# GpSimd's low-part subtractions in pieces of 512 columns

## The chip, the core and the metric

The kernel runs on one core of one Trainium2 chip. The metric is the device time of one execution in microseconds (us); the number to predict is the median over several runs. The engines are called as in the profile: PE is TensorE's matmul, PEld its weight load, DVE is VectorE, ACT is ScalarE, POOL is GpSimd, and SP issues the DMAs.

## What is computed

Two decoder layers over 1024 tokens of 1024 features, in float32. The first layer's mixer selects 256 keys for each token with an indexer (top-k) and attends to them through a latent; the second is a sliding-window attention with grouped keys. Each layer also reads a memory of 256 tokens through a cross-attention, and is followed by a gated MLP with a short causal convolution.

```python
for i in range(DEPTH):                                   # 2 layers: mixer A, then mixer B
    h = rmsnorm(x, g_mix[i])
    mix, q_mem = mixer_a(h, ...) if kind == 0 else mixer_b(h, ...)
    mem_o = memory_cross_attention(q_mem, mem_n, w_mem_kv[i])
    x = x + jnp.concatenate([mix, mem_o], axis=-1) @ w_out
    x = x + conv_glu_ffn(rmsnorm(x, g_ffn[i]), f_w_up[i], f_conv_w[i], f_conv_b[i], f_w_down[i])
return rmsnorm(x, g_final)
```

## The kernel before

Everything lies with features on the 128 partitions and tokens along the columns, in two halves of 512 tokens (`HT`). Float32 accuracy comes from splitting: a value is rounded to `float32r` by ACT (the high part, a copy), and the low part is value minus high part. A product is then three matmuls (`mm3`, lines 256 to 258): high by high, high by low, low by high. The third, L258, reads the low part of the weights as the stationary operand, 128 columns at a time.

The weights come as units of 128 x 1024 (`ukv`: 896). `Weights._split` (lines 92 to 108) takes a loaded unit, has ACT copy the high part (L99) and POOL subtract (L100), some units ahead of their use (`SPLIT`). For the second layer's up projection the units are factors of 128 x 512 that DVE forms first; their copy is L105, their subtraction L106. A projection (`proj`) reads a unit in eight blocks of 128 columns, three matmuls for each; the down products read two units together, four pairs of blocks one after the other into PSUM tiles of 128 x 1024, and each is added to the residual by DVE (L852 in the first layer, L1040 in the second), which frees the PSUM tile.

Other subtractions on POOL: `norm_apply`'s inner `lower` (L447), where every second block of the normalized activations goes to POOL and the others to DVE; `store_hl` (L555) for the rotated queries; `gate` (L806) and `keep` (L941) in the MLPs, each of 512 columns; and `split` (L273).

DVE has the rest: the sums of squares of a norm (`fold_in`, L393 and L401: folds of 1024 columns into 512, and additions of blocks), whose result PE multiplies with ones (L413); Newton's steps for the reciprocal root (L416 to L428, on 128 x 4); the normalization (L455); and the top-k search of the first layer, a bisection over bits with very small operations (L1229 to L1272, on 128 x 4 or smaller) between counts over the scores (L1224).

The program is issued by hand in one order (`manual_schedule`): each engine runs its instructions in the order in which Python issued them. Work in the background is interleaved by estimated times (`tick`, `add_bg`); those estimates don't depend on how many instructions a subtraction is made of. All DMAs are issued on SP's queue. All 128 x 4 KB tiles (`t4`) come from one pool of 51 buffers.

Of the kernel before, what the change touches and what calls it, by code (L numbers as in the profile page):

```python
# [59 lines left out]
class Weights:  # L60
# [30 lines left out]
    def _split(self):  # L91
        i = self.ready
        while self.loaded < self.need[i]:
            self._load()
        nc, t = self.t.nc, self.t
        if len(self.order[i]) == 2:
            raw, w = self.raw.pop(self.need[i] - 1)
            hi, lo = t.t4(1024, dt=R32), t.t4(1024, dt=R32)
            nc.scalar.copy(hi[:, :w], raw[:, :w])  # L99
            nc.gpsimd.tensor_tensor(lo[:, :w], raw[:, :w], hi[:, :w].bitcast(F32), op=OP.subtract)  # L100
            self.hl[i] = (hi, lo)
        else:
            src = self._factor(i)
            hl = t.t4(2, HT, dt=R32)
            nc.scalar.copy(hl[:, 0], src)  # L105
            nc.gpsimd.tensor_tensor(hl[:, 1], src, hl[:, 0].bitcast(F32), op=OP.subtract)  # L106
            self.hl[i] = (hl[:, 0], hl[:, 1])
        self.ready += 1

# [64 lines left out]
class Trunk:  # L174
# [85 lines left out]
    def evac_hl(self, hi, lo, src, scale=1.0):  # L260

        nc = self.nc
        if scale == 1.0:
            nc.scalar.copy(hi, src)  # L264
            nc.vector.tensor_tensor(lo, src, hi.bitcast(F32), op=OP.subtract)  # L265
        else:
            nc.scalar.mul(hi, src, scale)
            nc.vector.scalar_tensor_tensor(lo, src, scale, hi.bitcast(F32), op0=OP.mult, op1=OP.subtract)

    def split(self, hi, lo, src):  # L270

# [167 lines left out]
    def norm_apply(self, rb, x, gain, per, out, pace=2500, ease=False, keep=None, engs=None):  # L439


        nc, hs = self.nc, []

        def lower(i, h, hi):
            lo = self.t4(1024, dt=R32).rearrange("p (k n) -> p k n", k=per)
            eng = engs or (nc.gpsimd if i % 2 else nc.vector)
            eng.tensor_tensor(lo, h, hi.bitcast(F32), op=OP.subtract)  # L447
            out.append((hi, lo))

        late = []  # L450
        for i in range(len(x) + 1):
            if i < len(x):
                h = self.t4(1024).rearrange("p (k n) -> p k n", k=per)
                for k in range(per):
                    nc.vector.scalar_tensor_tensor(h[:, k], x[i][:, k], gain[:, i * per + k:i * per + k + 1], rb,  # L455
                                                   op0=OP.mult, op1=OP.mult)
                hs.append(h)
                if keep:
                    keep(i, h)
                yield pace  # L460
            if late:
                lower(*late.pop())
            if i:
                h = hs.pop(0)
                hi = self.t4(1024, dt=R32).rearrange("p (k n) -> p k n", k=per)
                nc.scalar.copy(hi, h)
                late.append((i - 1, h, hi))
                if not ease:
                    lower(*late.pop())
        if late:  # L470
            yield 1200
            lower(*late.pop())
# [77 lines left out]
    def store_hl(self, key, src, dst, scale=1.0, in_sbuf=False):  # L550

        hi, lo = self.t4(2, HT, dt=R32)[:, :, :src.shape[-1]], self.t4(2, HT, dt=R32)[:, :, :src.shape[-1]]
        if in_sbuf:
            self.nc.scalar.copy(hi, src)
            self.nc.gpsimd.tensor_tensor(lo, src, hi.bitcast(F32), op=OP.subtract)  # L555
        else:
            self.evac_hl(hi, lo, src, scale)
        for e in range(2):
            self.store(key, dst(0, e), hi[:, e].bitcast(F32))
            self.store(key, dst(1, e), lo[:, e].bitcast(F32))  # L560
# [213 lines left out]
    def ffn(self, l, halves, fold=1, last=None, then=None):  # L774
# [24 lines left out]
        def gate(f, hf, uv, b):  # L799
            u, v = uv  # L800
            nc.vector.tensor_tensor(u, v, b, op=OP.mult)
            if f % 2 == 0:
                G[hf, f // 2] = (self.t4(2, HT, dt=R32), self.t4(2, HT, dt=R32))
            gh, gl = G[hf, f // 2]
            nc.scalar.copy(gh[:, f % 2], u)
            nc.gpsimd.tensor_tensor(gl[:, f % 2], u, gh[:, f % 2].bitcast(F32), op=OP.subtract)  # L806

        def up(f):
            wa = self.w.get(f"up{l}", f)
# [109 lines left out]
    def ffn_up(self, l, h, ready, B, n_std, near_end):  # L919

        nc, name = self.nc, f"up{l}"

        def conv(f, hf, a):
            cw, prev = self.conv[:, l, f], self.prev_a[:, l, f]
            u = self.t4(HT)
            nc.scalar.activation(u, a, AF.Identity, bias=cw[:, 3:4], scale=cw[:, 2:3])
            nc.vector.scalar_tensor_tensor(u[:, 1:], a[:, :HT - 1], cw[:, 1:2], u[:, 1:], op0=OP.mult, op1=OP.add)
            nc.vector.scalar_tensor_tensor(u[:, 2:], a[:, :HT - 2], cw[:, 0:1], u[:, 2:], op0=OP.mult, op1=OP.add)  # L930
            if hf == 0:
                nc.scalar.copy(prev, a[:, HT - 2:])
            else:
                nc.vector.scalar_tensor_tensor(u[:, 0:1], prev[:, 1:2], cw[:, 1:2], u[:, 0:1], op0=OP.mult, op1=OP.add)
                nc.vector.scalar_tensor_tensor(u[:, 0:2], prev, cw[:, 0:1], u[:, 0:2], op0=OP.mult, op1=OP.add)
            return u

        def keep(f, hf, u):
            t = self.t4(2, HT, dt=R32)
            nc.scalar.copy(t[:, 0], u)  # L940
            nc.gpsimd.tensor_tensor(t[:, 1], u, t[:, 0].bitcast(F32), op=OP.subtract)  # L941
            self.store("G", self.G_d[f][hf], t.bitcast(F32))

        for hf in range(2):
            while not ready(hf):
                self.tick(100)
            for f in range(n_std):
                a, b = self.psB(), self.psB()
                self.proj(a, self.w.get(name, f), h[hf])
                u = conv(f, hf, a)  # L950
                wb = self.w.get(name, NF + f)
                if hf and f == n_std - 1:
                    self.w.SPLIT = self.AHEAD
                self.proj(b, wb, h[hf])
                nc.scalar.activation(u, u, AF.Silu)
                nc.vector.tensor_tensor(u, u, b, op=OP.mult)
                keep(f, hf, u)
                del a, b, u, wb
        b11, b21, b22 = h[0][:2], h[0][2:], h[1][2:]
        del h[:]  # L960
        while len(B[3]) < 2:
            self.tick(100)

        def group(f):
            A, Bk, C = self.psB(), self.psS()[:, :HT], self.psB()
            k = [0]

            def mul(out, b, start):
                w = self.w.get(name, (f, NF + f), k[0])
                k[0] += 1  # L970
                self.product(out, w, b, start)

            tt = nc.vector.tensor_tensor
            cu, vc, ab = self.t4(2, HT), self.t4(2, HT), self.t4(2, HT)
            c1, u2, v, c22, c12, c21 = cu[:, 0], cu[:, 1], vc[:, 0], vc[:, 1], ab[:, 0], ab[:, 1]
            mul(A, b11, True)
            nc.scalar.copy(c1, A)
            yield
            mul(Bk, B[1], True)
            tt(u2, c1, Bk, op=OP.add)  # L980
            yield
            mul(C, B[0], True)
            tt(v, c1, C, op=OP.add)
            yield
            mul(A, b21, False)
            ua = conv(f, 0, A)
            yield
            mul(Bk, B[2], False)
            tt(c22, v, Bk, op=OP.add)
            nc.scalar.activation(ua, ua, AF.Silu)  # L990
            yield
            mul(C, b22, False)
            tt(c12, u2, C, op=OP.add)
            ub = conv(f, 1, c12)
            yield
            mul(Bk, B[3], False)
            tt(c21, c1, Bk, op=OP.add)
            tt(ua, ua, c21, op=OP.mult)
            nc.scalar.activation(ub, ub, AF.Silu)
            yield  # L1000
            keep(f, 0, ua)
            tt(ub, ub, c22, op=OP.mult)
            yield
            keep(f, 1, ub)

        before = iter(())
        for f in range(n_std, NF):
            g = group(f)
            for _ in range(7):
                next(g)  # L1010
                next(before, None)
            for _ in before:
                pass
            before = g
            near_end(f)
        for _ in before:
            pass
        self.w.SPLIT = Weights.SPLIT
# [1108 lines left out]
```

## Time and profile before

| | |
|---|---|
| median of 3 runs | 2682.89 us (2682.31 to 2684.56) |
| profiled execution, its own time | 2683.7 us |
| its span, first to last instruction | 2681.9 us |
| mean granted TensorE clock | 0.965 |
| DVE busy | 1775.3 us (66%) |
| ACT busy | 1190.1 us (44%) |

The profile is of one execution. Busy times are unions of an engine's instructions. A timeline merges instructions that follow each other with the same line and shape (x2, x3) and gives the time from the first one's start to the last one's end; "[4.11 <-DVE t L852]" means that the engine had been idle for 4.11 us before it, and that the wait was ended by the instruction of line 852 on DVE that writes a tile t. pS and pB are PSUM tiles, t is any of the SBUF tiles.

### The profile page before, as it was taken

To read this page: it belongs to the slowest core of one execution; us is meant where nothing else is said; L and a number is where in the kernel's file an instruction comes from. 1 tells how busy PE (TensorE), PEld (TensorE's weight loads), DVE (VectorE), ACT (ScalarE), POOL (GpSimd) and SP (SyncE) were. 2 spreads that over 40 slices of the span, in tenths; PEclk is the share of its full clock that TensorE was granted. 3 is DMA by queue.
4 is the path that set the end of the run, shared out by engine and by line. 5 is a ranking of instruction groups with operands and counts; after the bars stand their busy time and mean duration, and the time that the engine had idled before them with its cause. 6 is when DMAs were issued, how large, how long until landed. Compare 5 with 4: busy or idle time off the path is not lost. (4 is left out here: it accounts for less than half of the span.)

```text
span 2681.9 us, 33704 instructions
## 1 busy us (share of the span) xinstructions
PE 2480.3 (92%) x11912; PEld 2066.6 (77%) x11912; DVE 1775.3 (66%) x3016; ACT 1190.1 (44%) x2214; POOL 1344.5 (50%) x942
## 2 busy tenths in 40 slices
PE   6789889988998999989999989999989999999997
PEld 5667667867776789877778878878867888887886
DVE  7899997876679556664663361588786565655446
ACT  4444456644442555433333333678744444442103
POOL 4544343444554643336756555656645666664203
PEclk8899999998998999999999999999999999999998
DMA  5444345422222254232323327453144323249301
GB/s 198 145 150 133 127 135 209 148 72 88 84 85 74 77 201 126 87 118 79 104 84 110 102 75 235 136 187 115 67 157 157 120 101 124 97 145 365 134 24 63
DMA packets 122233, 338.00 MB, mean 126 GB/s; under 512 B 13136, under 2 KB 30032, under 8 KB 122064
## 3 DMA queue, kind: packets, MB, share of 16 engines
q1 hardware_dynamic: 122064, 335.85, 37.4%
q8 instruction: 94, 1.54, 0.2%
q14 instruction: 75, 0.61, 0.1%
HBM read 262.40 MB, written 73.40 MB: 125 GB/s over the span
## 5 line engine op out<-in xcount | busy, mean ns | idle before, releaser
L100 POOL TENSOR_TENSOR t<-t,t 128x1024 fp32r<-128x1024 f32 (+1 forms) x292 | 720.6, 2483 | 483.1 <-ACT t L99 328.9
L256 PE MATMUL pB<-t,t 128*128 128x512 f32 (+3 forms) x1824 | 683.1, 375 | 12.0 <-DVE t L766 4.7
L257 PE MATMUL pB<-t,t 128*128 128x512 f32 (+3 forms) x1824 | 680.3, 373 | 11.6 <-DVE t L447 9.4
L258 PE MATMUL pB<-t,t 128*128 128x512 f32 (+3 forms) x1824 | 680.1, 373 | 8.9 <-POOL t L100 8.9
L256 PE MATMUL pS<-t,t 128*128 128x512 f32 (+1 forms) x1460 | 578.7, 396 | 59.5 <-DVE t L852 28.0
L258 PE MATMUL pS<-t,t 128*128 128x512 f32 (+1 forms) x1460 | 572.7, 392 | 13.1 <-POOL t L100 13.1
L257 PE MATMUL pS<-t,t 128*128 128x512 f32 (+1 forms) x1460 | 572.6, 392 | 0.8 <-DVE t L498 0.8
L256 PEld LDWEIGHTS pB<-t,t 128*128 128x128 f32 (+1 forms) x1824 | 347.0, 190 | 73.3 <-DVE t L766 5.0
L257 PEld LDWEIGHTS pB<-t,t 128*128 128x128 f32 (+1 forms) x1824 | 347.0, 190 | 71.9 <-DVE t L447 10.7
L258 PEld LDWEIGHTS pB<-t,t 128*128 128x128 f32 (+1 forms) x1824 | 346.9, 190 | 71.0 <-POOL t L100 10.8
L256 PEld LDWEIGHTS pS<-t,t 128*128 128x128 f32 x1460 | 284.1, 195 | 122.1 <-DVE t L852 37.7
L99 ACT CAST t<-t 128x1024 fp32r<-128x1024 f32 (+1 forms) x292 | 296.9, 1043 | 101.8 <-PE pS L258 44.4
L258 PEld LDWEIGHTS pS<-t,t 128*128 128x128 f32 x1460 | 283.3, 194 | 74.1 <-POOL t L100 17.5
L257 PEld LDWEIGHTS pS<-t,t 128*128 128x128 f32 x1460 | 284.0, 195 | 53.0 <-DVE t L498 1.6
L106 POOL TENSOR_TENSOR t<-t,t 128x512 fp32r<-128x512 f32 x133 | 177.4, 1347 | 136.9 <-ACT t L105 136.9
L265 DVE TENSOR_TENSOR t<-pB,t 128x512 fp32r<-128x512 f32 (+3 forms) x248 | 149.8, 623 | 84.3 <-ACT t L264 81.8
L264 ACT CAST t<-pB 128x512 fp32r<-128x512 f32 (+3 forms) x248 | 126.5, 535 | 151.8 <-PE pB L258 82.5
L1040 DVE TENSOR_TENSOR t<-t,pS 128x1024 f32<-128x1024 f32 (+1 forms) x92 | 108.0, 1174 | 124.0 <-PE pS L258 123.8
L796 POOL TENSOR_TENSOR t<-t,t 128x512 f32<-128x512 f32 x44 | 57.2, 1299 | 201.8 <-ACT t L795 201.8
L852 DVE TENSOR_TENSOR t<-t,pS 128x1024 f32<-128x1024 f32 x88 | 106.5, 1217 | 65.2 <-PE pS L258 65.0
L1415 POOL TENSOR_SCALAR t<-t,st 128x128 f32<-128x128 f32 (+3 forms) x64 | 47.9, 751 | 141.6 <-DVE st L1414 78.9
L787 ACT ACTIVATE t<-t,conv 128x512 f32<-128x512 f32 x44 | 35.9, 816 | 175.8 <-DVE t L786 175.8
(239 smaller groups left out, 3405.3 us busy)
## 6 DMA issues: line engine op xcount, KB each, us to landing
t<-in_up SPq DMA_DIRECT2D x138, 512.0 KB
t<-in_down SPq DMA_DIRECT2D x66, 512.0 KB
G_d<-t SPq DMA_DIRECT2D x44, 512.0 KB
t<-G_d SPq DMA_DIRECT2D x44, 512.0 KB
t<-in_a_in SPq DMA_DIRECT2D x42, 512.0 KB
t<-in_b_in SPq DMA_DIRECT2D x28, 512.0 KB
t<-in_a_out SPq DMA_DIRECT2D x20, 512.0 KB
t<-x_d SPq DMA_DIRECT2D x20, 512.0 KB
```

What stands on the lines that cost most here:

```text
L99: nc.scalar.copy(hi[:, :w], raw[:, :w])
L100: nc.gpsimd.tensor_tensor(lo[:, :w], raw[:, :w], hi[:, :w].bitcast(F32), op=OP.subtract)
L106: nc.gpsimd.tensor_tensor(hl[:, 1], src, hl[:, 0].bitcast(F32), op=OP.subtract)
L256: mm(out, a[0], b[0], start=start, stop=False, skip_group_check=again)
L257: mm(out, a[0], b[1], start=False, stop=False, skip_group_check=again)
L258: mm(out, a[1], b[0], start=False, stop=stop, skip_group_check=again)
L264: nc.scalar.copy(hi, src)
L265: nc.vector.tensor_tensor(lo, src, hi.bitcast(F32), op=OP.subtract)
L796: nc.gpsimd.tensor_tensor(v, v, rb[0], op=OP.mult)
L852: nc.vector.tensor_tensor(x[dp][:, :, t], x[dp][:, :, t], S, op=OP.add)
L1040: nc.vector.tensor_tensor(xp, xp, S, op=OP.add)
L1415: nc.gpsimd.tensor_scalar(Pt[:, :n], Pt[:, :n], st[:, 2:3], 1.0, op0=OP.mult, op1=OP.mult)
```

## The change

A helper `rest` makes GpSimd's subtraction in pieces of at most 512 columns, along the last dimension of the tile. Five of the six places that made one instruction on POOL call it now; where the tile has two dimensions of columns (`lower`, `store_hl`), it is called for each index of the first. `split` stays as it was. Where the instruction was 512 wide already (`gate`, `keep`, the factors of the second layer's up projection), one piece is made, as before. In `lower` the other blocks still go to DVE.

```diff
@@ _split
-            nc.gpsimd.tensor_tensor(lo[:, :w], raw[:, :w], hi[:, :w].bitcast(F32), op=OP.subtract)
+            t.rest(lo[:, :w], raw[:, :w], hi[:, :w])
...
-            nc.gpsimd.tensor_tensor(hl[:, 1], src, hl[:, 0].bitcast(F32), op=OP.subtract)
+            t.rest(hl[:, 1], src, hl[:, 0])
@@ Trunk
+    PIECE = 512
+
+    def rest(self, lo, src, hi):
+        if self.w.order is None:
+            return
+        for i in range(0, src.shape[-1], self.PIECE):
+            s = slice(i, min(i + self.PIECE, src.shape[-1]))
+            self.nc.gpsimd.tensor_tensor(lo[:, s], src[:, s], hi[:, s].bitcast(F32), op=OP.subtract)
@@ norm_apply
-            eng = engs or (nc.gpsimd if i % 2 else nc.vector)
-            eng.tensor_tensor(lo, h, hi.bitcast(F32), op=OP.subtract)
+            if engs is None and i % 2:
+                for k in range(per):
+                    self.rest(lo[:, k], h[:, k], hi[:, k])
+            else:
+                nc.vector.tensor_tensor(lo, h, hi.bitcast(F32), op=OP.subtract)
@@ store_hl
-            self.nc.gpsimd.tensor_tensor(lo, src, hi.bitcast(F32), op=OP.subtract)
+            for e in range(2):
+                self.rest(lo[:, e], src[:, e], hi[:, e])
@@ gate
-            nc.gpsimd.tensor_tensor(gl[:, f % 2], u, gh[:, f % 2].bitcast(F32), op=OP.subtract)
+            self.rest(gl[:, f % 2], u, gh[:, f % 2])
@@ keep
-            nc.gpsimd.tensor_tensor(t[:, 1], u, t[:, 0].bitcast(F32), op=OP.subtract)
+            self.rest(t[:, 1], u, t[:, 0])
```

## Rows read from the trace of the kernel before

**Rows 1.** The page's first part: busy us, share of span, instructions.

```profile
PE 2480.3 (92%) x11912; PEld 2066.6 (77%) x11912; DVE 1775.3 (66%) x3016; ACT 1190.1 (44%) x2214; POOL 1344.5 (50%) x942
```

**Rows 2.** Busy us by stretch: PE, PEld, DVE, ACT, POOL, granted clock, DMA, GB/s.

```profile
200.00:300.00 100.00, 92.55 (x460) 76.42 (x458) 92.58 (x190) 48.16 (x91) 37.18 (x15) 1.00 0.45 143
1400.00:1500.00 100.00, 100.00 (x470) 83.91 (x469) 36.04 (x53) 32.63 (x43) 58.45 (x31) 1.00 0.33 106
```

**Rows 3.** Waits of PE: who waited for whom; us in all, times, longest.

```profile
PE pS L256 <- DVE t L852: 28.0, 14, 6.0
...
PE pS L413 <- DVE t L401: 17.0, 3, 7.2
...
PE pS L258 <- POOL t L100: 13.1, 9, 2.3
...
PE pB L258 <- POOL t L100: 8.9, 4, 4.4
PE pB L413 <- DVE t L401: 8.5, 2, 8.3
```

**Rows 4.** The costliest groups, line 100: busy us, mean ns, idle before, releaser.

```profile
L100 POOL TENSOR_TENSOR t<-t,t 128x1024 fp32r<-128x1024 f32 (+1 forms) x292 | 720.6, 2483 | 483.1 <-ACT t L99 328.9
```

**Rows 5.** Timelines of POOL, DVE, PE, 834 to 845: start, us, instruction, idle before.

```profile
834.96 9.32 POOL L100 TENSOR_TENSOR t<-t,t 128x1024 fp32r<-128x1024 f32 x4
...
834.98 2.37 DVE L1270 TENSOR_TENSOR ti<-tc 128x1 int32<-128x1 int32 x1
837.39 2.30 DVE L1271 TENSOR_TENSOR ti<-ti 128x1 int32<-128x1 int32 x1
839.72 2.27 DVE L1272 TENSOR_TENSOR ti<-ti,tc 128x1 int32<-128x1 int32 x1
...
843.23 1.22 DVE L852 TENSOR_TENSOR t<-t,pS 128x1024 f32<-128x1024 f32 x1
...
844.50 0.79 PE L256 MATMUL pS<-t,t 128*128 128x512 f32 x1 [4.11 <-DVE t L852]
```

**Rows 6.** Timelines of POOL, DVE and PE around a fold, 545 to 557.

```profile
546.59 8.43 POOL L100 TENSOR_TENSOR t<-t,t 128x1024 fp32r<-128x1024 f32 x3 [5.21 <-ACT t L99]
...
545.46 4.62 DVE L401 TENSOR_TENSOR t<-t,t 128x1024 f32<-128x1024 f32 x2
550.11 5.45 DVE L393 TENSOR_TENSOR t<-t 128x512 f32<-128x512 f32 x2
555.60 0.69 DVE L401 TENSOR_TENSOR t<-t,t 128x512 f32<-128x512 f32 x1
...
556.34 0.80 PE L413 MATMUL pS<-ones,t 128*128 128x1 f32 x3 [7.23 <-DVE t L401]
```

**Rows 7.** Timeline of POOL: two subtractions of 512 columns in a row.

```profile
2102.01 2.54 POOL L106 TENSOR_TENSOR t<-t,t 128x512 fp32r<-128x512 f32 x2
```

**Rows 8.** Timelines of POOL and PE, 597 to 602: two weights waited for.

```profile
597.34 4.66 POOL L100 TENSOR_TENSOR t<-t,t 128x1024 fp32r<-128x1024 f32 x2
...
599.74 0.50 PE L258 MATMUL pS<-t,t 128*128 128x512 f32 x1 [1.99 <-POOL t L100]
...
602.05 0.79 PE L258 MATMUL pS<-t,t 128*128 128x512 f32 x1 [1.35 <-POOL t L100]
```

**Rows 9.** Timelines of DVE and PE at 1738.6: one tile, two halves.

```profile
1738.64 0.69 DVE L265 TENSOR_TENSOR t<-pB,t 128x512 fp32r<-128x512 f32 x1 [1.68 <-ACT t L264]
...
1738.66 0.38 PE L737 MATMUL pB<-t,t 128*128 128x256 f32 x1
1739.39 0.39 PE L737 MATMUL pB<-t,t 128*128 128x256 f32 x1 [0.34 <-DVE t L265]
```

**Rows 10.** Timeline of DVE: one operation of a Newton step.

```profile
67.40 7.07 DVE L427 SCALAR_TENSOR_TENSOR st<-st 128x4 f32<-128x4 f32 x1
```

**Rows 11.** Timeline of DVE beside two subtractions, 685.9 to 690.6.

```profile
685.95 2.29 DVE L1250 TENSOR_SCALAR ti<-tc 128x4 int32<-128x4 f32 x1
688.28 2.27 DVE L1253 TENSOR_TENSOR ti<-ti 128x4 int32<-128x4 int32 x1
```

## The prediction

> **What bounds the kernel now.** I read the page's first part, then the waits of PE alone, then, around the largest of them, the timelines of DVE and POOL side by side. PE is busy for 92% of the span and POOL for half of it [rows 1]; from 1400 to 1500 us PE does not idle at all and runs at the full granted clock [rows 2]. So 314 more POOL instructions are no matter in themselves: there is room for them. What the change can move is the time that PE waits, 202 us (the span less PE's busy time [rows 1]), and there POOL's subtractions stand in two places. First openly: PE waits 13 times, 22.0 us in all, for a low part of a weight (L258 behind L100) [rows 3]. Then hidden, behind DVE: PE waits 28.0 us for the additions of L852, which free a PSUM tile, and 25.5 us for the last fold of a norm's squares (L413 behind L401) [rows 3], and in both DVE itself had been stopped by POOL.
>
> How DVE is stopped is to be seen in [rows 5]: while four subtractions run (9.32 us, 2.33 each), three DVE operations on 128x1 elements take 2.37, 2.30 and 2.27 us. Each ends where a subtraction ends: it can't run beside one, is let in when one is over, and then the next subtraction runs. In [rows 6] the same happens to the folds: two of 128x512 take 5.45 us, where the last one, with no subtraction beside it, takes 0.69. A DVE operation with one of its operands in PSUM does not suffer: the L852 of [rows 5] runs beside the fourth subtraction, which lasts to 844.28, in 1.22 us, and PE starts right behind it.
>
> **The price of a cut.** A subtraction of 1024 columns takes 2.33 us in a row of its like [rows 5], two of 512 take 2.54 [rows 7]: a cut adds 0.2 us at most. Going by starts the pair costs less, since each starts a little before the one in front ends; I keep 0.2. Line 100 issues 292 [rows 4], eight of them for the 896-wide units of `ukv`, which are cut into 512 and 384. By the code L447 on GpSimd is issued 12 times, of which ten become two pieces and the two of the memory's norm become four of 256 each, and the six of line 555 become two each. That is 292 + 10 + 6 + 6 = 314 more instructions and 63 us more of POOL at the most, on an engine that is idle for half the span [rows 1]. Lines 106, 806 and 941 were 512 wide already and stay as they are. No DMA is moved, no allocation and no order: the pieces stand where the one instruction stood. The stores that wait for line 555's low parts wait for both pieces; nothing on PE waits for them soon (the store is put off by a set time, the load comes a stage later), so I cost that at nothing, with 0.2 us for each if the cover were gone.
>
> The pieces also add waits on PE, since the matmuls that read columns 512 and on now wait for a second piece. A wait that has been met costs nothing that rows show: PE begins a new unit of weights every 24 matmuls, with its waits on ACT and POOL, and the second of [rows 2] still shows 100 us of 100 busy with 470 matmuls. If it cost, 314 such waits at one tenth of a matmul's spacing (100 / 470 = 0.213 us) would be 7 us; I take 0.
>
> **Part A: PE waits for a low part.** The first matmul to read it needs columns 0 to 127. Does it wait for the first piece alone? The trace has the like in [rows 9]: of one tile, the high half is read by the first L737 while DVE is still writing the low half (from 1738.64, for 0.69 us), and the second L737, which reads that half, waits for DVE. So a wait goes by the part of a tile that is read, and I take it that pieces are told apart too. The first piece is then there 2.33 - 1.27 = 1.06 us earlier. The second follows 1.27 us after it; in a projection its first reader stands 12 matmuls (2.6 us) behind, which covers it, and also if DVE gets one operation in between (an L401 of 1.2 us: 2.5 in all, though only just). In the down products the cover is twice that. In [rows 8] two weights are needed one after the other, and the first piece of the second is the third of four: 3 x 1.27 = 3.8 us after the start against 4.66, so 0.85 is saved for both waits together. So the 22.0 us in 13 waits can give at most 11 x 1.06, some 12 us; several are shorter than that or run into a later wait for DVE, which takes the gain back. I take 8, with 2 to 12 as bounds.
>
> **Part B: the folds.** When m DVE operations in a row each need a subtraction's end, and R subtractions stand in a row, the last of them is through after min(m, R) x 2.33 us before and min(m, 2R) x 1.27 after. For one operation this saves 1.06; for three against four, 7.0 - 3.8 = 3.2; for two against one it loses 0.2, and for four against two 0.4. This is what sets the gain: only a chain shorter than the number of pieces gains, because a longer one has to see all of POOL's work pass anyway. The fold of [rows 6] has four (L401, L393, L393, L401) against three. The three blocked ones ended 0.5 us behind the third subtraction; after the change four turns of 1.27 us and DVE's own turns between them (8.43 - 3 x 2.33 = 1.4 for three, 1.9 for four) are 7.0 us from 546.59, so 553.6 + 0.5 for the last against 556.3 now: 2.2 us of PE's 7.23. There are five such waits of PE [rows 3]; four have this pattern: 4 x 2.2 = 8.8, with 4 to 16 as bounds (16: 3.2 for each of five).
>
> **Part C: evictions behind blocked small operations.** At 844 us [rows 5] three operations against four subtractions delay L852: 3.2 of a wait of 4.11 go. The pattern of [rows 11], two blocked ones followed by two more of the same chain, with two subtractions, is m = 4 against R = 2 and gains nothing. For the other 13 waits of L852 I take 2 us together, as two with a single blocked operation in front (1.06 each): POOL's instructions of lines 796 and 806, 512 wide and unchanged, can stand beside the rest as well. Sum 5 us of 28.0, bounds 0 to 14 (half of all).
>
> **Sum.** 8 + 8.8 + 5 = 21.8, less 2 us for second halves that come late: some 20 us. On the profiled execution's 2683.7 us (span 2681.9 and 1.8 around it) that gives 2663.7; it lies 0.8 us over the median of the runs, so I forecast 2663. The parts' upper bounds sum to 42 us, which is 2641.
>
> **The rivals.** (1) Time-sharing gives it all back: where DVE has a full queue of operations that POOL excludes, m is large everywhere, and the gains of B and C are 0 or -0.2 per chain. From 200 to 300 us DVE is busy for 92.58 us of 100 [rows 2], and I count nothing there. If the folds too turn out to be followed by something that is late anyway (ACT's cast of weights), only A less 2 us is left, and part of that is lost to later waits: 2678 to 2685, about 2681. For it: most waits of PE are for DVE, and its whole work is the same. Against it: in [rows 6] the fold is the last that PE waits for.
>
> (2) No hand-over at a cut. [Rows 10] has one DVE operation, L427, of 7.07 us, which sat through two 32-partition operations and two subtractions without being let in once. If back-to-back pieces leave no gap as those did, DVE gains nothing, and A alone stands: about 2677, with a POOL that is 0.2 us later for each cut. Against it: [rows 5], [rows 6] and [rows 11], where DVE got in at the end of each. The Trainium skill (GPSIMD Engine Reference, 2.1 Instruction dispatch) says that each of the engine's eight cores starts on the next instruction as soon as its own share of this one is done; by that rule the cores could run apart and never leave the gap. The trace agrees only where an instruction of 32 partitions stood in front.
>
> (3) Slower: the low parts come later. Every cut is a place where DVE gets in, and its operation (0.5 us in a fold of 512, up to 1.2 in one of 1024) then stands between POOL's halves. If PE's wait is for the whole tile after all, each of the 13 waits [rows 3] grows by 0.2 + 0.5 to 1.2 us, 9 to 18 us; it decides as soon as the second half comes more than 12 matmuls (2.6 us) behind the first or is waited for at once. With B and C gone to rival 1 that is 2692 to 2701, about 2695. For it: where DVE makes the right factors (L894 and L902, both 1024 wide) it does so beside the splits of the weights that PE needs next. Against it: [rows 9].
>
> **How the numbers follow.** The forecast, 2663 with its own range of 2645 to 2675, has 0.66; rival 1 has 0.16; rival 2 has 0.08; rival 3 has 0.10. The 8-in-10 range reaches down to a little over the sum of the upper bounds and up over rival 1: 2645 to 2686. Some 0.2% (5.4 us) is what a measurement of this kernel can tell from no change. Faster by more than that: 0.66, most of rival 2 (0.05) and a little of rival 1 (0.02): 0.73. Same: the rest of rivals 1 and 2, 0.16. Slower: rival 3 and a remnant, 0.11.
>
> **What will show it.** POOL's instructions should go from 942 to 1256 and its busy time up by 45 to 63 us. The three operations of [rows 5] should take 1.2 to 1.3 us each and the wait of 4.11 shrink below 1.5; PE's wait for the fold in [rows 6] should be near 5; the waits for L100 should fall from 22 to under 12 us with the first piece as the releaser. The stretch from 200 to 300 us should take the time it takes now. I am wrong if DVE operations of the old 2.3 us remain beside POOL pieces (rival 2), if L258's waits for L100 grow (rival 3), or if the waits shrink as said and the span does not, since then another wait took their place (rival 1).

## The result and the profile after

The change makes the kernel faster: 2654.2 us (2650.07 to 2655.39) against 2683.72 us for the kernel before on the same chip, a ratio of 0.9886 with a 95% interval of 0.9871 to 0.9902. That is 29.5 us, where I had forecast 20; the forecast was 2663, with 2645 to 2675 as its range. The profiled execution took 2653.0 us, with a span of 2651.2.

The lines of the code have moved. L100, L106, L447 (its part on POOL), L555, L806 and L941 all issue from L279 now; L447's part on DVE is L461, L455 is L469, L401 is L412, L393 is L404, L413 is L424, L852 is L867, L1250 is L1265, L1270 to L1272 are L1285 to L1287, and L788 is L803.

The page's first part of the kernel after (busy us, share of span, instructions), which answers [rows 1]:

```profile
PE 2472.4 (93%) x11912; PEld 2061.4 (78%) x11912; DVE 1755.7 (66%) x3016; ACT 1188.9 (45%) x2214; POOL 1419.6 (54%) x1256
```

The span fell by 30.7 us. This page splits that in two. PE's idle time (span less busy time) went from 201.6 to 178.8 us, 22.8 less; and PE's busy time fell by 7.9, for the same 11912 matmuls. DVE's busy time, which contains the time for which it is stopped, fell by 19.6 of 1775.3 us. How long DVE was stopped can be estimated from the traces: what each operation took beyond the shortest of its kind, counted from 0.15 us up, sums to 262 us before and 243 after. So DVE was stopped for nearly as long as before, only by shorter pieces and in other places: I take most of the gain to be one of order. POOL has 1256 instructions, as worked out, and 75 us more of busy time.

The waits of PE in the kernel after (who waited for whom; us in all, times, longest), which answer [rows 3]:

```profile
PE pS L256 <- DVE t L867: 25.6, 13, 6.9
...
PE pS L258 <- POOL t L279: 8.8, 6, 3.1
PE pS L424 <- DVE t L412: 8.7, 2, 4.9
...
PE pB L258 <- POOL t L279: 5.4, 3, 3.3
...
PE pB L424 <- DVE t L412: 2.3, 1, 2.3
PE pB L257 <- POOL t L279: 1.3, 2, 1.1
```

| | forecast | waits before | waits after | difference |
|---|---|---|---|---|
| Part A, L258 for a low part | 8 | 22.0 | 14.2 | 7.8 less |
| Part B, folds | 8.8 | 25.5 | 11.0 | 14.5 less |
| Part C, L852 / L867 | 5 | 28.0 | 25.6 | 2.4 less |
| all other idle time of PE | 2 more | 126.1 | 128.0 | 1.9 more |

So the idle time fell by 22.8 us, near the 20 of the sum, with Part B's waits shrinking by more and Part C's by less than I had said; PE's busy time is what the sum did not contain at all. A row of this table tells which waits became shorter, not what the cuts at that place are worth: the experiments show that waits move from one row to another.

The place of [rows 5] in the kernel after, timelines of POOL, DVE and PE (start, us, instruction, idle before):

```profile
816.60 10.46 POOL L279 TENSOR_TENSOR t<-t,t 128x512 fp32r<-128x512 f32 x8 [3.93 <-ACT t L820]
...
818.12 1.27 DVE L1285 TENSOR_TENSOR ti<-tc 128x1 int32<-128x1 int32 x1
...
819.43 1.20 DVE L1286 TENSOR_TENSOR ti<-ti 128x1 int32<-128x1 int32 x1
820.66 1.20 DVE L1287 TENSOR_TENSOR ti<-ti,tc 128x1 int32<-128x1 int32 x1
...
823.10 1.22 DVE L867 TENSOR_TENSOR t<-t,pS 128x1024 f32<-128x1024 f32 x1
...
824.37 0.51 PE L256 MATMUL pS<-t,t 128*128 128x512 f32 x1 [1.30 <-DVE t L867]
```

The three operations take half of their time and PE's wait is 1.30 us instead of 4.11. The fold of [rows 6] in the kernel after:

```profile
534.49 3.51 DVE L412 TENSOR_TENSOR t<-t,t 128x1024 f32<-128x1024 f32 x2
535.63 9.73 POOL L279 TENSOR_TENSOR t<-t,t 128x512 fp32r<-128x512 f32 x6 [4.54 <-ACT t L99]
...
538.04 3.31 DVE L404 TENSOR_TENSOR t<-t 128x512 f32<-128x512 f32 x2
541.38 1.63 DVE L412 TENSOR_TENSOR t<-t,t 128x512 f32<-128x512 f32 x1
...
543.07 1.86 PE L424 MATMUL pS<-ones,t 128*128 128x1 f32 x8 [4.89 <-DVE t L412]
```

The wait is 4.89 us, where 7.23 less 2.2 had been worked out. Two of the six pieces now end behind the fold; before, all three subtractions ran ahead of its end.

### The profile page after: what moved, and what is told of

Read it like the earlier page. It is cut to its first block, busy times and chain, and to the rows that moved or that the text cites. A ratio compares the mean times of both kernels' runs of the same rounds, so it can differ in the third digit from the quotient of the medians.

```text
span 2651.2 us, 34066 instructions
## 1 busy us (share of the span) xinstructions
PE 2472.4 (93%) x11912; PEld 2061.4 (78%) x11912; DVE 1755.7 (66%) x3016; ACT 1188.9 (45%) x2214; POOL 1419.6 (54%) x1256
## 5 line engine op out<-in xcount | busy, mean ns | idle before, releaser
L279 POOL TENSOR_TENSOR t<-t,t 128x512 fp32r<-128x512 f32 (+1 forms) x845 | 1134.1, 1372 | 705.5 <-ACT t L99 274.7
L256 PE MATMUL pB<-t,t 128*128 128x512 f32 (+3 forms) x1824 | 683.1, 374 | 10.6 <-DVE t L781 4.0
L258 PE MATMUL pB<-t,t 128*128 128x512 f32 (+3 forms) x1824 | 679.4, 372 | 5.4 <-POOL t L279 5.4
L256 PE MATMUL pS<-t,t 128*128 128x512 f32 (+1 forms) x1460 | 577.1, 395 | 56.4 <-DVE t L867 25.6
L258 PE MATMUL pS<-t,t 128*128 128x512 f32 (+1 forms) x1460 | 571.7, 392 | 9.0 <-POOL t L279 8.8
L258 PEld LDWEIGHTS pB<-t,t 128*128 128x128 f32 (+1 forms) x1824 | 346.7, 190 | 67.0 <-POOL t L279 6.7
L258 PEld LDWEIGHTS pS<-t,t 128*128 128x128 f32 x1460 | 282.5, 193 | 69.6 <-POOL t L279 13.5
L867 DVE TENSOR_TENSOR t<-t,pS 128x1024 f32<-128x1024 f32 x88 | 106.4, 1216 | 63.2 <-PE pS L258 63.1
L1239 DVE TENSOR_SCALAR_CACHE_REDUCE hit<-t,ti 128x384 bf16<-128x384 f32 (+5 forms) x136 | 111.4, 819 | 1.6
```

The source lines that it names most:

```text
L256: mm(out, a[0], b[0], start=start, stop=False, skip_group_check=again)
L258: mm(out, a[1], b[0], start=False, stop=stop, skip_group_check=again)
L279: self.nc.gpsimd.tensor_tensor(lo[:, s], src[:, s], hi[:, s].bitcast(F32), op=OP.subtract)
L867: nc.vector.tensor_tensor(x[dp][:, :, t], x[dp][:, :, t], S, op=OP.add)
L1239: nc.vector.tensor_scalar(hits("hit")[:, :(blks[i] + 1) * 128], wks[i], cand[:, i:i + 1].bitcast(F32), 0.0, op0=op, op1=OP.add, accum_out= ...
```

## The experiments

Each was compared with runs of the kernel before on the same chip.

**The pieces in the other order.** Columns 512 and on first, columns 0 to 511, which the first matmul reads, last. This takes Part A away and leaves the number and size of POOL's instructions as they are.

```diff
-        for i in range(0, src.shape[-1], self.PIECE):
+        for i in reversed(range(0, src.shape[-1], self.PIECE)):
```

> All pieces stay, but each subtraction makes its last 512 columns first. DVE is let in at the same places, so the folds and evictions keep their gain; PE's first reader of a low part (columns 0 to 127) now waits for the last piece. Theory (part A is a gain of its own, by the first piece alone): PE's waits for L100's low parts go from 14.2 us in the changed kernel back to 20 or more, and the kernel takes 8 to 12 us longer than the changed one: 2662 to 2667. Rival (PE waits for the whole tile anyway, the gain is all DVE's): no difference, 2651 to 2657.

Measured: 2657.78 us (2655.15 to 2660.08), ratio 0.9909 [0.9894, 0.9924], so 3.6 us over the change, with intervals that just overlap. Its waits of PE:

```profile
PE pS L256 <- DVE t L867: 21.0, 11, 4.5
PE pS L258 <- POOL t L279: 17.1, 9, 5.3
...
PE pB L258 <- POOL t L279: 9.2, 3, 5.5
```

The waits for a low part are 26.3 us against 14.2 (and 22.0 before the change), so the order of the pieces does decide when PE starts: a matmul waits for its own piece. But the span grew by only 2.2 us: PE's idle time is 182.8 against 178.8, so 8.1 of the 12.1 us came back out of other waits, 4.6 of them out of those for L867. Most of what the order saves here is waited for again a little later. I had expected the loss to be larger; the waits behaved as said, the time did not.

**The folds only, and all but the folds.** In the first, only the eleven weights that are split beside four of the folds are cut in two, and all else is whole, as in the kernel before; the second is the opposite.

```diff
-            t.rest(lo[:, :w], raw[:, :w], hi[:, :w])
+            t.rest(lo[:, :w], raw[:, :w], hi[:, :w], t.piece_of(i))
...
+    FOLD = (2, 3, 4, 62, 63, 64, 142, 143, 144, 259, 260)
+    def piece_of(self, i):
+        return 512 if i in self.FOLD else 1024      # the second kernel: 1024 if ... else 512
```

> Only the eleven weight subtractions that ran beside four folds of squares (three each at 25, 547 and 1168 us, two at 1969 us of the kernel before) are cut into 512; the other 281 of line 100 and those of the norms and the rotated queries are whole again. Theory (which chain stands behind a subtraction decides, not how many are cut): this alone gives the folds' 14.5 us, with some of the time that PE spends at half clock after them: 2664 to 2670. Rival (the gain comes from many small delays all over): under a twentieth of the gain, 2680 to 2684.

> The reverse of the one before: all subtractions are cut but those eleven. Theory: the folds' waits return to about 25 us in all, and 14 to 18 us of the gain are lost: 2668 to 2672. Rival (many small delays): as the changed kernel, 2651 to 2657.

Measured: folds only 2672.99 us (2671.63 to 2674.15), ratio 0.9963 [0.9951, 0.9976], 10.6 us less than before; all but the folds 2666.76 us (2661.22 to 2668.67), ratio 0.9934 [0.9921, 0.9948], 16.8 us less. The two add up to 27.4 of the 29.5 us, loosely, as the five runs of the second spread over 7.5 us. Both lie outside what I had expected: the folds alone give less, and leaving them out costs less. The folds' waits in the first kernel:

```profile
PE pS L430 <- DVE t L418: 12.3, 3, 4.9
PE pB L430 <- DVE t L418: 5.1, 1, 5.1
```

and in the second:

```profile
PE pS L430 <- DVE t L418: 14.3, 2, 7.2
PE pB L430 <- DVE t L418: 6.8, 1, 6.8
```

In all the folds' waits are 17.4 us in the first kernel and 21.1 in the second, against 25.5 before and 11.0 with the change. So the eleven cuts alone take 8.1 us off them. The other 303 take off 4.4 though they cut nothing beside these folds: the wait of 2.63 us at 1978 us is gone in the second kernel too, and PE comes to the first fold later.

Eleven cuts give over a third of the whole gain, and the other 303 the rest. PE's busy time did not fall with the folds only (2481.2 us, against 2480.3 before [rows 1]); in the trace of the second it did (2470.0), but that trace is of its fastest run, 5.5 us below the median.

**The weights before the first MLP only**, those that are split between some 35 and 545 us, without the folds'; here the prediction had counted nothing.

```diff
+    def piece_of(self, i):
+        return 512 if i < 62 and i not in self.FOLD else 1024
```

> Only the weights that are split from some 35 to 545 us of the kernel before are cut, without those at the folds; all else is whole. By the prediction nothing is to be had there (DVE is busy for 92.58 of 100 us from 200 to 300): 2681 to 2684. By the progress of PE, which gains 5.9 us between 135 and 395 us without a fold: 2675 to 2679.

Measured: 2680.34 us (2674.7 to 2683.58, 11 runs), ratio 0.9986 [0.9978, 0.9995]: 3.0 us less than before, between the two expectations. It is little, but not nothing. The change itself gained more in this stretch. If the start of the same matmul of PE is compared in the traces of before and after, the lead is 5.0 us at 141 us, 7.5 at 203, 9.0 at 309 and 11.1 at 392. The first 5.0 are mostly those of the first fold (at 70 us the kernel with the folds only leads by 3.8). One step of that, from 5.0 to 7.4, is not of the weights but of the normalized activations, to whose pieces on POOL I had given no gain: between 141 and 187 us the kernel with all but the folds, which cuts them too, gains 4.3 us, and the one that cuts only these weights 0.2. Before:

```profile
187.80 0.58 PE L257 MATMUL pB<-t,t 128*128 128x256 f32 x1 [7.03 <-DVE t L447]
```

and after:

```profile
180.40 0.51 PE L257 MATMUL pB<-t,t 128*128 128x256 f32 x1 [4.96 <-DVE t L461]
```

The low part that PE waits for is one that DVE makes, beside those of POOL, and I take it that shorter pieces let DVE through sooner.

**Two weights whole**, at the one place where the kernel after loses some of its lead (22.9 us at 861 us, 18.6 at 900), beside the end of the top-k.

```diff
+    def piece_of(self, i):
+        return 1024 if i in (110, 111) else 512
```

> As the change, but the two weights that are split from 850 to 859 us, beside the end of the first layer's top-k, are subtracted whole. There PE waits 7.28 us in three waits with the change and 4.12 us in three before it, and its lead over the kernel before falls from 22.9 to 18.6 us between 861 and 900 us. If the cuts cause these waits (DVE's 1024-wide operations get in between the pieces and the low part comes later), the time falls by about 3 to 4 us, to 2650. Rival: the lead is lost there whatever POOL does, since the same thing (the top-k's last operations) is awaited: within 1.5 us of 2654.

Measured: 2654.43 us (2651.78 to 2656.36), ratio 0.9894 [0.9881, 0.9907]; the same as the change. Two waits of PE there, with the cuts:

```profile
854.94 0.79 PE L258 MATMUL pS<-t,t 128*128 128x512 f32 x1 [3.14 <-POOL t L279]
858.82 0.79 PE L258 MATMUL pS<-t,t 128*128 128x512 f32 x1 [2.23 <-POOL t L279]
```

and with the two weights whole:

```profile
854.14 0.80 PE L258 MATMUL pS<-t,t 128*128 128x512 f32 x1 [4.21 <-POOL t L283]
857.43 0.80 PE L258 MATMUL pS<-t,t 128*128 128x512 f32 x1 [1.64 <-POOL t L283]
```

My reading of that place, that DVE's 1024-wide operations between the pieces delay the low part, falls: without the cuts the waits are as long. The lead is lost there either way.

**Smaller pieces.** 256 columns everywhere, 128 everywhere, and each of the two with 512 kept where it was 512 before the change (factors, `gate`, `keep`).

```diff
-    PIECE = 512
+    PIECE = 256        # or 128
...
+            t.rest(hl[:, 1], src, hl[:, 0], 512)          # the kernels that keep 512: here,
...
+            self.rest(gl[:, f % 2], u, gh[:, f % 2], 512) # in gate and in keep
```

> Pieces of 256 columns everywhere, the former 512-wide ones of the gate, the kept products and the factors among them. A piece of 256 takes 0.71 us in a row of its like, so four take 2.84 against 2.54 for two of 512. Theory (a chain of four DVE operations gets past four pieces, whatever their size): each of four folds comes 4 x (1.27 - 0.71) = 2.2 us earlier again and PE's first piece 0.5 us earlier, in all 4 to 13 us: 2641 to 2650; POOL's busy time rises by 130 to 170 us to about 1570, without a wait of PE for it. Rival (POOL's longer work is what the next wait is for): no better or slower, 2654 to 2670.

> All pieces of 128 columns (some 3800 instructions on POOL). If what counts is only how long one POOL instruction keeps DVE out, the step from 256 to 128 should give again about half of what 512 to 256 gave (41 us): near 2593, with POOL busy for some 1900 us. Rival: the fixed cost of an instruction (a pair of 512 takes 0.2 us more than a 1024, a piece of 256 takes 0.82 us where half of a 512 would be 0.69) now doubles the time of a low part, POOL falls behind ACT's copies and PE waits for L279 more than at 256 (7.1 us in 4 waits): 2620 to 2650. I hold the rival for a little likelier, with the total near 2615.

> Pieces of 256 for the weights, the normalized activations and the queries, while the subtractions that were 512 wide before the change (factors, gate, keep) stay 512. If the gain of 256 over 512 comes from the first layer and the folds, as the progress of PE suggests (33 of its 41 us stand by 827 us), the time is 2615 to 2622. Rival: the factors and the MLPs' own subtractions carry half of it: 2630 to 2636.

> Pieces of 128 for the weights, the normalized activations and the queries; the subtractions that were 512 wide before the change (factors, gate, keep) stay 512. With 128 everywhere PE fell behind the version of 256 by 25.6 us between 1998 and the end, evenly along the second layer's up projection, where POOL makes factors and was busy for 87.5 of 100 us. If the factors alone do that, this takes 2632 to 2642 (2665.5 less some 25 to 30). Rival: POOL is too slow in 128 for the whole-width weights of the second layer too (17 us lost between 1150 and 1550): then no better than 2650 at best, as the loss is only partly of the factors.

| pieces | us | ratio | POOL busy (instructions) | DVE busy | PE idle |
|---|---|---|---|---|---|
| 1024 (before) | 2683.7 | 1 | 1344.5 (942) | 1775.3 | 201.6 |
| 512 (after) | 2654.2 | 0.9886 | 1419.6 (1256) | 1755.7 | 178.8 |
| 256 | 2613.12 | 0.9741 [0.9727, 0.9754] | 1587.0 (2091) | 1708.0 | 149.5 |
| 256, 512 kept | 2614.4 | 0.9742 [0.9729, 0.9755] | 1545.7 (1870) | 1708.1 | 147.3 |
| 128, 512 kept | 2622.58 | 0.9784 [0.9771, 0.9797] | 1762.2 (3100) | 1709.0 | 159.6 |
| 128 | 2665.53 | 0.9934 [0.9921, 0.9948] | 1881.2 (3763) | 1771.5 | 186.2 |

Pieces of 256 give another 41 us, more than the change itself, and are the fastest kernel here; it makes no difference whether the 512-wide ones are cut too. The chain of [rows 11] shows one part of where this comes from. In the kernel after:

```profile
667.69 6.21 POOL L279 TENSOR_TENSOR t<-t,t 128x512 fp32r<-128x512 f32 x5 [1.51 <-ACT t L820]
...
669.07 1.17 DVE L1265 TENSOR_SCALAR ti<-tc 128x4 int32<-128x4 f32 x1
670.27 1.20 DVE L1268 TENSOR_TENSOR ti<-ti 128x4 int32<-128x4 int32 x1
671.50 1.20 DVE L1261 SCALAR_TENSOR_TENSOR ti<-ti 128x4 int32<-128x4 int32 x1
672.74 1.19 DVE L1244 TENSOR_SCALAR ti<-ti 128x4 int32<-128x4 int32 x1
```

and with pieces of 256:

```profile
641.40 6.97 POOL L279 TENSOR_TENSOR t<-t,t 128x256 fp32r<-128x256 f32 x10 [1.51 <-ACT t L820]
...
642.89 0.67 DVE L1265 TENSOR_SCALAR ti<-tc 128x4 int32<-128x4 f32 x1
643.60 0.66 DVE L1268 TENSOR_TENSOR ti<-ti 128x4 int32<-128x4 int32 x1
644.29 0.66 DVE L1261 SCALAR_TENSOR_TENSOR ti<-ti 128x4 int32<-128x4 int32 x1
644.99 0.66 DVE L1244 TENSOR_SCALAR ti<-ti 128x4 int32<-128x4 int32 x1
```

With whole subtractions two of these four are stopped for 2.3 us each, and the four take some 5.0 us (685.95 to 690.95). With halves all four are stopped, for 1.2 us each: 4.9 us, so nothing is gained, as the prediction's rule says for a chain of four against two. With quarters there are more pieces than links, and the four take 2.8 us. The halves leave the many chains of four in the top-k as they were; the quarters are past that bound. So the rule of the prediction contained this, and my expectation of 2641 to 2650 did not use it. But these chains are hardly most of the 41 us. The time for which the top-k's small operations were stopped, estimated as above, is 63 us with 1024, 63 with 512 and 55 with 256, while that of all of DVE fell from 243 to 213 between the last two, most at the normalization (L469: 29 to 13). And the waits for L867, before which these chains stand, fell by 4.1 us only, from 25.6 to 21.5. By the start of the same matmuls, the kernel of 256 leads the one of 512 by 6.7 us at 187 us of the kernel before, when the top-k begins, by 30.3 at 827 and by 39.0 at the end. What each place gives was not tried apart.

With 128 everywhere most of the gain is lost again, and more than I had expected in either case (2665.53 us, against 2620 to 2650 for the slower one). In the second layer's up projection, pieces of 256 (busy us: PE, PEld, DVE, ACT, POOL; granted clock, DMA share, GB/s):

```profile
2140.00:2240.00 100.00, 100.00 (x442) 82.79 (x442) 58.40 (x89) 44.65 (x82) 72.09 (x96) 1.00 0.31 108
```

and pieces of 128:

```profile
2140.00:2240.00 100.00, 96.79 (x423) 78.74 (x422) 67.31 (x86) 41.75 (x77) 87.51 (x182) 1.00 0.28 106
```

PE, which never stopped there, now idles for 3 us of 100, and does 423 matmuls in place of 442. PE's waits there, 3.2 us in five, are all for ACT's copy of a factor (L105), none for POOL. With the factors, `gate` and `keep` left at 512 this stretch is whole again: PE is busy for 100.00 of 100 us, with 443 matmuls. That kernel, at 2622.58 us, is faster than both of my expectations for it: what it leaves at 512 accounts for 43 of the 52 us between 256 and 128 everywhere. But both kernels of 128 lose time elsewhere too. POOL and DVE at 1254 us, 128 everywhere:

```profile
1253.95 13.02 POOL L279 TENSOR_TENSOR t<-t,t 128x128 fp32r<-128x128 f32 x31
...
1256.74 10.78 DVE L803 SCALAR_TENSOR_TENSOR t<-t,conv 128x511 f32<-128x511 f32 x1 [0.94 <-ACT t L802]
1267.56 0.75 DVE L804 SCALAR_TENSOR_TENSOR t<-t,conv 128x510 f32<-128x510 f32 x1
```

Here is rival 2: L803, an operation of 0.75 us, stands ready at 1256.74 and is not let in at one of the 24 cuts that follow; it runs when POOL's row of 31 pieces is over. In the up projection the same happens to L121, one of the operations that make a factor: its median over 19 is 2.306 us, against 0.682 with 512 or 256, and in 18 of the 19 at least four ends of pieces pass without letting it in. As PE waits there for the copy of the factor, this points to L121 rather than to POOL's busy time. I counted such cases in the traces: DVE operations that took 0.15 us or more longer than the shortest of their kind, and those among them that an end of a low-part subtraction passed without letting them in. A kind is an operation with its shapes and tiles, and some of the counted ones stood beside another instruction of POOL (31 of the 176 before). They are 3 of 176 before, 4 of 269 after, 19 of 407 with 256, 49 of 445 with 128 and 512 kept, and 76 of 526 with 128 everywhere. So two things can turn the curve at 128: POOL's fixed cost, and cuts at which nobody gets in. I did not separate their shares.

**128 for the first 62 weights, then 256.** The trace of 128 everywhere led the one of 256 by 4.6 us at 566 us.

```diff
+    def piece_of(self, i):
+        return 128 if i < 62 else 256
```

> Pieces of 128 for the first 62 units of weights (until some 545 us of the kernel before), 256 for all other subtractions. With 128 everywhere PE led the version of 256 by 4.6 us at 566 us, before it fell behind. If what is gained before the MLP is kept, the time is 2606 to 2610. Rival: it is given back at the next wait for something else (the top-k's counts): 2612 to 2615, the same as 256.

Measured: 2617.02 us (2615.92 to 2619.76), ratio 0.9765 [0.9752, 0.9778]. Nothing is kept. The expected lead did not even form: the same matmul starts 0.7 us earlier than with 256 at 542 us and 2.1 us later at the end. This kernel does not repeat the early stretch of 128 everywhere, as its normalized activations are cut into 256; whether that took the lead away was not tried.

## Why the prediction was right, and where its sizes were off

The time, 2654.2 us, is in the range, 9 us below the forecast. The mechanism held: DVE gets in at the cuts, and PE's waits shrink. That the idle time came out at 22.8 us for 20 is in part luck, since terms that were off in opposite directions made it up.

**The bound and the price.** That POOL has room and PE's waits carry the gain held: 22.8 of the 30.7 us of the span are idle time of PE. The price of a cut on an idle DVE was right too: rows of pieces give 6.21 / 5 = 1.24 us for 512, 6.97 / 10 = 0.70 for 256 and 13.02 / 31 = 0.42 for 128, so a cut adds about 0.15 us (2 x 1.24 - 2.33 with [rows 5], 2 x 0.70 - 1.24, 2 x 0.42 - 0.70). The Trainium skill (GPSIMD Engine Reference, 3.1 Elementwise — side-by-side cycle accounting) gives about 156 ns for the start of one instruction on VectorE, and names further steps for GpSimd without a number; the 0.15 us measured here for GpSimd is no more than that. What was off is POOL's busy time, 75 us more where at most 63 were forecast: the mean of a 512-wide piece is 1.38 us, so a pair takes 2.76 against the 2.48 of [rows 4], I take it because DVE's operations now stand between some of the pieces: 683 of the 827 lie within 10% of the shortest and take 1.29 us, the others up to 2.9.

**Part A** was right in the waits (7.8 for 8, by the first piece as releaser; the wait goes by the part of the tile, as [rows 9] let expect), and too large in the time. The kernel with the pieces in the other order has 12.1 us more of these waits and is 3.6 us slower, so I put Part A's 7.8 us of waits at some 3.6 us of time at most. The sign that I had named, under 12 us of these waits, was missed (14.2), and did not go with a term of 8 either. The prediction had said that "several ... run into a later wait for DVE, which takes the gain back", and had taken that off the upper bound only.

**Part B** came out near its sum, 8.8, and not by its pattern. With the folds' cuts alone these waits fell by 8.1 us and the time by 10.6; the 14.5 of the table contains what the other cuts did. The rule was right, but I gave all folds the pattern of [rows 6]. In the kernel with the folds only the first wait lost 3.2 us, the second 2.3, the third 3.3, and the fourth grew by 0.9: four times 2.2 was right in the sum partly by luck. The first fold of the kernel is a chain of three against three subtractions. Before:

```profile
25.17 8.48 POOL L100 TENSOR_TENSOR t<-t,t 128x1024 fp32r<-128x1024 f32 x3 [11.07 <-ACT t L99]
25.98 5.46 DVE L393 TENSOR_TENSOR t<-t 128x512 f32<-128x512 f32 x2
31.48 2.71 DVE L401 TENSOR_TENSOR t<-t,t 128x512 f32<-128x512 f32 x1
34.25 1.86 PE L413 MATMUL pB<-ones,t 128*128 128x1 f32 x8 [8.34 <-DVE t L401]
```

and after:

```profile
24.93 8.23 POOL L279 TENSOR_TENSOR t<-t,t 128x512 fp32r<-128x512 f32 x5 [10.40 <-ACT t L99]
25.75 3.37 DVE L404 TENSOR_TENSOR t<-t 128x512 f32<-128x512 f32 x2
29.15 1.63 DVE L412 TENSOR_TENSOR t<-t,t 128x512 f32<-128x512 f32 x1
30.84 1.05 PE L424 MATMUL pB<-ones,t 128*128 128x1 f32 x8 [2.33 <-DVE t L412]
```

The three operations take 5.0 us (25.75 to 30.78) in place of 8.2 (25.98 to 34.19). This is the 3.2 us that the prediction had worked out for three against four and then kept for the upper bound. The wait lost 6.0 us in all in the kernel after; the rest of that PE had spent elsewhere, since it came to the wait 2.6 us later (28.5 against 25.9).

**Part C** was too large by the waits: 2.4 us for 5, though its one named place gave 2.8 of the forecast 3.2. For the other waits of L852 I had taken 2 us, and they gave none: one pattern in front of them is that of [rows 11], which halves don't shorten. These waits also take up what is saved elsewhere: they are 31.7 us with the folds only and 21.0 with the pieces in the other order, so 2.4 is no price of the cuts alone.

**What the sum left out** is PE's busy time, 7.9 us. The mean granted clock rose from 0.965 to 0.970. Between full speed (2.4 GHz) and half (1.2 GHz) that is a share of 7.0% of the span at the lower level before and 6.0% after; by the traces it is 186 and 160 us. The lower level stands with long waits: in both traces each of its 29 stretches has a wait of PE of 1 us or more in it or shortly before it. The first matmul after the 4.11 us of [rows 5] lasts 0.79 us, where most of the same shape last 0.39; the one after the 1.30 us that are left of it lasts 0.51. So I take it that a wait that goes takes with it some of the slow matmuls behind it, which a sum over waits doesn't see.

**"From 200 to 300 us ... I count nothing there"** was nearly right for the weights (3.0 us for the whole stretch up to 545 us in the kernel that cuts only those), and wrong for the pieces of the normalized activations, to which I had given no gain. From 203 to 309 us the kernel after gained 1.5 us.

**The rivals.** Rival 1 was right in its premise, since DVE was stopped for nearly as long as before (243 us for 262), and not in its conclusion, as the folds and the eviction of [rows 5] came sooner. Rival 3 falls: L258's waits for low parts shrank. Rival 2 does not hold at 512, where DVE was passed over 4 times of 269, and does at 128. The rule of the Trainium skill that I had named with it (GPSIMD Engine Reference, 2.1 Instruction dispatch: a core starts on the next instruction once its own share is done) would fit those rows, in which POOL never leaves a gap; at 1024, 512 and 256 the traces speak against that consequence of it in nearly all cases, and no run here shows the cores apart.

## What to carry to other kernels

Where GpSimd stops VectorE, the length of one GpSimd instruction matters more than GpSimd's total: halving it costs 0.15 us for each cut and shortens a chain of stopped operations as soon as there are more pieces than links in the chain, so count the links (here three or four) before choosing the size, and try the next smaller size too. Look for the other end of the curve in the same traces: GpSimd near 90% busy in a stretch, or one VectorE operation that lasts through a whole row of pieces. When waits are summed for a forecast, sort them by their own pattern rather than giving all the one that was looked at, look for the terms that move into each other, and add what PE loses at its lower clock behind each.

## What the hardware showed that I had not expected

VectorE is not always let in between two GpSimd instructions that contend with it. With pieces of 1024 or 512 columns it nearly always is (3 of 176 and 4 of 269 of the operations counted above were passed over); with 128 columns 76 of 526 were passed over, one of them by 24 pieces, for 10.78 us. What decides it stays open. And an operation on four columns or one (`128x4`, `128x1`), which takes 0.16 or 0.17 us by itself, is stopped for as long as any other: 2.3, 1.2 and 0.66 us with pieces of 1024, 512 and 256.
